# Mixing layer: mask adds and sums of squares moved from GpSimd to VectorE, rotated keys copied by ScalarE

## The chip, the cores and the metric

The kernel runs on one core of a Trainium2 chip. The metric is the device time of one execution in microseconds (us); the median of several runs counts. A core has five engines that each work through a queue of their own in order: TensorE (PE in the profile, its weight loads PEld), VectorE (DVE), ScalarE (ACT), GpSimd (POOL) and SyncE (SP). Transfers between the chip's main memory and the on-chip buffers run on 16 DMA engines; here SyncE issues nearly all of them (the weights, queue q1), ScalarE a few small tables (q10), and GpSimd the rest (q0).

## The reference, cut to what matters

The program is two transformer blocks in float32 over 256 tokens of width 1024. The first block, with its experts, is not touched. The second is a feed-forward layer, a mixing layer and a second feed-forward layer. The mixing layer, where the change lies, computes

```python
z = rms_norm_2(h, mix_pre_g[l]) @ w_in[l]
q_na, k_na, v_na, c_q, c_kv, k_rope = jnp.split(z, split_at, axis=-1)
o_na = neighbourhood_attention(q_na, k_na, v_na, na_rpb[l])      # 8 heads of 64
o_mla = latent_attention(c_q, c_kv, k_rope, ...)                 # 8 heads of 64 + 32 rotated
mixed = concat([rms_norm_2(o_na, g1), rms_norm_2(o_mla, g2)]) @ w_out[l]
h = h + rms_norm_2(mixed, mix_post_g[l])
...
bias = rpb[:, row_off, col_off]                    # in neighbourhood_attention
bias = jnp.where(col_mask, bias, NEG_INF)          # the mask
s = einsum(q, k) * D ** -0.5 + bias
...
k_rot = apply_rope(k_rope, cos, sin)               # in latent_attention: one key for all heads
s = (einsum(qn, k_nope) + einsum(qr, k_rot)) * scale
```

## The kernel before, in words

Every matrix product is made of three matmuls: both operands are split into a rounded high part and a low part (H and L in the names), and HH, LH and HL are summed (lines 116 to 118). ScalarE makes the high parts of weights (wH) and VectorE the low parts (wL), just ahead of TensorE, from three buffers each. Tokens come in two halves, tt = 0 and 1, of 128.

The mixing layer is the function mix. In the order of the code: small tables are loaded (gains, rope tables, the window table win of 128x64 that holds 0 or -1e30); then for each of four pairs of heads, hp, a bias table G of 128 x (2 heads x 6 x 64) is gathered from rpb in four loads of GpSimd's queue and the window is added to it in place on GpSimd (line 1758). The first three G have buffers of their own, the fourth lies in the buffer of a row that the feed-forward layer before it uses last. Then z for its last 416 columns (pslin from za and zb, the preloaded weights, into zr); late, the factor of the row norm of each half, which reaches TensorE through diag and psrr; the values vn from w_in columns (L1559 for their low parts); the norms of the two latent parts (rstd chains of small VectorE steps, then xh); the products with mla_w_uq (wuq) and mla_w_ukv (wukv); the rotation (rope, on VectorE), whose shared key kr GpSimd copies to 8 heads in mqk (line 1828). Then three streams are woven: the projections of q_na and k_na (pslt), the latent attention pairs, and the neighbourhood pairs (near), in which TensorE adds G to the scores by a matmul with ident (line 1876). The function attend does softmax and output of a pair; its last steps square the output on ScalarE into sqt (line 2029) and, from the second pair on, add it to the running sum sq on GpSimd (line 2031). After the last pair four small matmuls (pssq) reduce sq to the norm factors of the output.

What sets the order: a scheduler walks the instructions by priority, mostly the order of the code, with a model of its own of when each is ready, and writes down a fixed queue for every engine except SyncE, whose loads stay in the order of the code. So an instruction that is written late in the code can be placed early where the model sees its engine free. At run time each engine takes its queue strictly in order and waits at each instruction for semaphores. A DMA signals its end on one of eight counters for loads of SyncE and ScalarE (DMAHW0 to 7) or one of eight for loads of GpSimd (DMASW0 to 7), taken in turn; a load can't be issued before the earlier load on the same counter has landed. The window table, on ScalarE's queue, has the counter of wukv, on SyncE's.

Of the kernel before, what the change touches and what calls it, by code (L numbers as in the profile page):

```python
# [15 lines left out]
ALU = mybir.AluOpType  # L16
# [4 lines left out]
P = 128  # L21
# [83 lines left out]
class Net:  # L105
# [1621 lines left out]
    def mix(self):  # L1727
        nc, tc, a = self.nc, self.tc, self.a
        H, L = self.H, self.L
        with ExitStack() as es:  # L1730
# [11 lines left out]
            win = pool.tile([P, 64], F32, name="win")  # L1742
# [3 lines left out]
            biases = []  # L1746
            for hp in range(4):
                if hp < 3:
                    G = pool.tile([P, 2, 6, 64], F32, tag="G", name="G", bufs=3)
                else:  # L1750

                    G = self.pc.tile([P, D], F32, tag="row", name="G")[:, 0:768].rearrange("p (a r c) -> p a r c", a=2, r=6)
                for j, half in itertools.product(range(2), range(2)):
                    src = bass.AP(tensor=rpb.tensor, offset=rpb.offset + (2 * hp + j) * 465 + (5 - half) * 31 - 48,
                                  ap=[[1, 64], [31, 6], [1, 64]])
                    nc.gpsimd.dma_start(G[half * 64:half * 64 + 64, j], src)
                G = G.rearrange("p a r c -> p (a r) c")
                nc.gpsimd.tensor_tensor(G, G, win[:, None, :].to_broadcast([P, 12, 64]), op=ALU.add)
                biases.append(G)
            W = a["w_in_2"]  # L1760

            def into(t, n, late=False):
# [25 lines left out]
            for tt in range(2):  # L1788
                t = pool.tile([P, P], F32, tag="diag", name="diag", bufs=2)
# [15 lines left out]
            q, kk = qk[:, 0], qk[:, 1]  # L1805
# [17 lines left out]
            for tt in range(2):  # L1823
                c, s = rope[:, tt, 0], rope[:, tt, 1]
                self.rope(q[:, tt, :, 64:96], q[:, tt, :, 64:96], c, s, 8)
                kr = pool.tile([P, 1, 32], F32, tag="kr", name="kr", bufs=2)
                self.rope(kr, zr[:, tt, None, 384:416], c, s, 1)
                nc.gpsimd.tensor_copy(kk[:, tt, :, 64:96], kr.to_broadcast([P, 8, 32]))

            def projections():  # L1830
                for t, c0, scale, rev in ((qn, 0, 0.125, 64), (kn, 512, 1.0, 0)):
# [6 lines left out]
            sq = [pool.tile([P, S], F32, tag=f"sq{i}", name=f"sq{i}") for i in range(2)]  # L1838
# [25 lines left out]

            def near(hp):
                G = biases[hp]
                yield
                ss = [self.ps.tile([P, 2, S], F32, tag="wk", name="psna") for _ in range(2)]
                for tt in range(2):
                    for j in range(2):  # L1870
                        hs = slice(j * 64, j * 64 + 64)
                        nc.tensor.matmul(ss[j][:, tt], qn[hs, hp, tt * P:(tt + 1) * P], kn[hs, hp, :],
                                         start=tt == 0, stop=False, skip_group_check=True)
                for j in range(2):
                    for tt in range(2):
                        nc.tensor.matmul(ss[j][:, tt], self.ident, G[:, 6 * j + 2 - 2 * tt:6 * j + 6 - 2 * tt, :],
                                         start=False, stop=tt == 1, skip_group_check=True)
                yield
                yield from self.attend(ss, [self.att_p() for _ in range(2)], 1.0, lambda kb, j: vn[:, kb, (2 * hp + j) * 64:(2 * hp + j) * 64 + 64],
                                       hp, *outs[0], gout[0], sq[0], 64)  # L1880
# [6 lines left out]
            def latent_out():  # L1887
                for j in range(2):
                    yield from self.linear_steps(*outs[1], 4, ws[0][j], 512,
                                                 lambda tt, ps: nc.scalar.copy(z1[tt][j], ps), "ln", 2)  # L1890

            weave([projections(), wait(5), latent_out()], [latent(0), latent(2), near(0), near(2)],
                  [wait(2), latent(1), latent(3), near(1), near(3)])

            parts = []
# [11 lines left out]
            r = None  # L1907
            for tt in range(2):
                z0 = {}
                for j in ((0, 1), (1, 0))[tt]:  # L1910
# [6 lines left out]
                    if r is None:  # L1917
# [8 lines left out]
                        with tc.high_priority():  # L1926
                            nc.vector.tensor_scalar(v, ps, 4.0 / 512, 4 * EPS, op0=ALU.mult, op1=ALU.add)
                            r = self.rstd_wide(pool, v)
# [57 lines left out]
    def attend(self, s, p, scale, v, hp, oH, oL, g, sq, rev):  # L1986

        nc, pool = self.nc, self.pa  # L1990
        m = pool.tile([P, 2, 4], F32, tag="attm", name="attm", bufs=2)
        for j in range(2):
            nc.vector.tensor_reduce(m[:, j, 0:2], s[j], axis=AX.X, op=ALU.max, negate=True)
        if scale != 1.0:
            nc.vector.tensor_scalar(m[:, :, 0:2], m[:, :, 0:2], scale, None, op0=ALU.mult)
        yield
        for j in range(2):
            for tt in range(2):
                nc.scalar.activation(p[j][:, tt], s[j][:, tt], AF.Exp, bias=m[:, j, tt:tt + 1], scale=scale,
                                     accum_out=m[:, j, 2 + tt:3 + tt])  # L2000
        nc.vector.reciprocal(m[:, :, 2:4], m[:, :, 2:4])
        for j in range(2):
            for tt in range(2):
                nc.vector.tensor_scalar(p[j][:, tt], p[j][:, tt], m[:, j, 2 + tt:3 + tt], None, op0=ALU.mult)
        yield
        pT = []
        for j in range(2):
            pt = self.ps.tile([P, 2, S], F32, tag="wk", name="pspt")
            for kb in range(2):
                for tt in range(2):  # L2010
                    nc.tensor.transpose(pt[:, kb, tt * P:(tt + 1) * P], p[j][:, tt, kb * P:(kb + 1) * P], self.ident)
            t = pool.tile([P, 2, S], F32, tag="attT", name="attT", bufs=4)
            nc.scalar.copy(t, pt)
            pT.append(t)
        yield
        po = self.ps.tile([P, S], F32, tag="wk", name="pspo")
        for kb in range(2):
            for j in range(2):
                nc.tensor.matmul(po[j * 64:j * 64 + 64], v(kb, j), pT[j][:, kb], start=kb == 0, stop=kb == 1,  # L2019
                                 skip_group_check=True)  # L2020
        t = sq if hp == 0 else pool.tile([P, S], F32, tag="attT", name="sqt", bufs=4)
        h, lo, o, o2 = oH[:, hp], oL[:, hp], po, t
        if rev:
            o, h, lo, o2 = (u.rearrange("p (g r) -> p g r", r=rev) for u in (o, h, lo, o2))
            o = o[:, :, ::-1]
        gk = g[:, hp:hp + 1]
        nc.scalar.activation(h, o, AF.Copy, scale=gk)
        nc.vector.scalar_tensor_tensor(lo, o, gk, h.bitcast(F32), op0=ALU.mult, op1=ALU.subtract)
        nc.scalar.activation(o2, o, AF.Square)
        if hp:  # L2030
            nc.gpsimd.tensor_tensor(sq, sq, t, op=ALU.add)
        yield


# [47 lines left out]
```

## Time and profile before

| what | value |
|---|---|
| median of 3 runs | 1282.73 us (1282.36 to 1283.06) |
| profiled execution, own time | 1284.1 us |
| its span, first to last instruction | 1282.3 us |
| TensorE busy | 1199.6 us, 94% |
| VectorE busy | 704.2 us, 55% |
| ScalarE busy | 550.6 us, 43% |
| GpSimd busy | 36.2 us, 3%, 43 instructions |
| granted clock of TensorE | 0.990 of full speed |
| main memory read | 349.46 MB, 273 GB/s over the span |

The mixing layer takes the stretch from about 950 to 1085 us of the span, after the experts (to about 720 us) and the first feed-forward layer of the second block. Times in the rows below count from the span's start. A TensorE row that reads "[1.30 <-DVE diag L1790]" says that TensorE stood idle for 1.30 us before this instruction and that VectorE's instruction of line 1790, which writes diag, ended the wait.

### The profile page before, as it was taken

The page shows a single profiled execution, that of the slowest core. Times are in us where ns is not written, and L with a number is a line of the kernel's source. Part 1 is how long each engine was busy: PE and PEld are TensorE (multiplying, and loading weights), DVE is VectorE, ACT ScalarE, POOL GpSimd, SP SyncE. Part 2 cuts the span into 40 slices and gives each one's busy share as a digit, 9 for nine tenths or more (in the row PEclk, how much of TensorE's full clock was granted, in tenths as well). Part 3 has the DMA queues.
Part 4 walks back from the last instruction along what each step waited for, and adds up shares of the span by engine and source line. Part 5 has one row for each costly group of instructions (what it writes and reads, how often), then busy time and mean ns, then how long its engine had stood idle before and what let it go on. Part 6 is the DMA issues. An engine that isn't in the chain of part 4 may idle for free. (4 is left out here: it accounts for less than half of the span.)

```text
span 1282.3 us, 19860 instructions
## 1 busy us (share of the span) xinstructions
PE 1199.6 (94%) x7213; PEld 817.4 (64%) x7213; DVE 704.2 (55%) x1570; ACT 550.6 (43%) x1056; POOL 36.2 (3%) x43
## 2 busy tenths in 40 slices
PE   5999999999899899899879989999998998999997
PEld 3885788775354344335335447888876976788885
DVE  3565888774343233133323257667769767666664
ACT  3466765642121111011112146556635675555652
POOL 0000000000000000000000000000024000000000
PEclk9999999999999899899999999999999999999999
DMA  9886767789999999999999994953397114195510
GB/s 332 273 289 209 286 209 269 259 318 406 402 409 408 407 408 409 409 408 409 408 407 409 403 330 154 322 197 133 136 267 155 34 64 134 66 367 186 187 66 33
DMA packets 155140, 351.85 MB, mean 274 GB/s; under 512 B 14688, under 2 KB 69920, under 8 KB 155040
## 3 DMA queue, kind: packets, MB, share of 16 engines
q1 hardware_dynamic: 152816, 347.25, 73.1%
q0 software_dynamic: 1328, 3.16, 1.9%
q8 instruction: 58, 0.95, 0.3%
q14 instruction: 42, 0.34, 0.1%
q10 hardware_dynamic: 896, 0.15, 0.1%
HBM read 349.46 MB, written 1.06 MB: 273 GB/s over the span
## 5 line engine op out<-in xcount | busy, mean ns | idle before, releaser
L1337 PE MATMUL psgu<-wgu,xg 128*32 128x512 f32 x1600 | 215.1, 610 | 32.8 <-DMA wgu<-in_w_up_e_dram 32.0
L1337 PEld LDWEIGHTS psgu<-wgu,xg 128*32 128x32 f32 x1600 | 64.4, 112 | 175.5 <-issue 147.9
L1559 DVE SCALAR_TENSOR_TENSOR wL<-wgu,ffn_pre_g,wH 128x512 fp32r<-128x512 f32 x160 | 119.0, 751 | 72.5 <-ACT wH L1558 68.5
L1558 ACT ACTIVATE wH<-wgu,ffn_pre_g 128x512 fp32r<-128x512 f32 x160 | 114.2, 724 | 78.2 <-PE psgu L117 71.9
L116 PE MATMUL psgu<-wH,Hc 128*128 128x512 f32 x320 | 126.2, 394 | 0.0
L118 PE MATMUL psgu<-wL,Hc 128*128 128x512 f32 x320 | 124.9, 390 | 0.0
L117 PE MATMUL psgu<-wH,Lc 128*128 128x512 f32 x320 | 124.7, 390 | 0.0
L1344 DVE SCALAR_TENSOR_TENSOR act<-act,ws,psgu 128x256 f32<-128x256 f32 x25 | 12.0, 481 | 188.4 <-ACT act L1343 188.4
L1361 PE MATMUL psdn<-wdn,aT 128*32 128x512 f32 x800 | 93.4, 595 | 3.5 <-DVEq L1096 2.0
L1343 ACT ACTIVATE act<-psgu 128x256 f32<-128x256 f32 x25 | 9.6, 384 | 200.7 <-PE psgu L1337 200.7
L125 ACT CAST wH<-gt 128x512 fp32r<-128x512 f32 x61 | 37.7, 618 | 117.3 <-DVE gt L1197 106.0
L126 DVE TENSOR_TENSOR wL<-win,wH 128x512 fp32r<-128x512 f32 x80 | 54.0, 688 | 32.2 <-ACT wH L125 30.4
L118 PEld LDWEIGHTS psgu<-wL,Hc 128*128 128x128 f32 x320 | 60.1, 188 | 12.7
L117 PEld LDWEIGHTS psgu<-wH,Lc 128*128 128x128 f32 x320 | 60.1, 188 | 12.2
L116 PEld LDWEIGHTS psgu<-wH,Hc 128*128 128x128 f32 x320 | 60.1, 188 | 12.0
L126 DVE TENSOR_TENSOR wL<-gt,wH 128x512 fp32r<-128x512 f32 x61 | 42.2, 692 | 41.6 <-ACT wH L125 41.5
L125 ACT CAST wH<-win 128x512 fp32r<-128x512 f32 x80 | 48.2, 617 | 32.5 <-PE pslt L118 17.1
L1361 PEld LDWEIGHTS psdn<-wdn,aT 128*32 128x32 f32 x800 | 24.7, 109 | 53.6 <-issue 44.3
L1311 ACT ACTIVATE xg<-psga,sh,gs 128x256 f32<-128x256 f32 (+1 forms) x52 | 28.8, 556 | 66.1 <-PE psga L1310 66.1
L126 DVE TENSOR_TENSOR wL<-wdn,wH 128x512 fp32r<-128x512 f32 x64 | 44.1, 693 | 22.2 <-ACT wH L125 11.7
L125 ACT CAST wH<-wdn 128x512 fp32r<-128x512 f32 x64 | 39.5, 620 | 27.3 <-PE fy L117 18.8
L1309 PE MATMUL psga<-Pt,xH 128*128 128x256 f32 (+1 forms) x208 | 51.1, 288 | 0.0
(548 smaller groups left out, 2525.2 us busy)
## 6 DMA issues: line engine op xcount, KB each, us to landing
wgu<-in_w_gate_e_dram SPq DMA_DIRECT2D x128, 512.0 KB, 12.0
wgu<-in_w_up_e_dram SPq DMA_DIRECT2D x128, 512.0 KB, 12.0
wdn<-in_w_down_e_dram SPq DMA_DIRECT2D x62, 1024.0 KB, 12.1
wgu<-in_ffn_w_gu_dram SPq DMA_DIRECT2D x88, 512.0 KB, 6.7
win<-in_w_in_dram SPq DMA_DIRECT2D x26, 1024.0 KB, 12.2
wada<-in_w_ada_dram SPq DMA_DIRECT2D x24, 1024.0 KB, 7.7
wdn<-in_ffn_w_down_dram SPq DMA_DIRECT2D x22, 1024.0 KB, 9.2
wout<-in_w_out_dram SPq DMA_DIRECT2D x8, 1024.0 KB, 14.3
```

What stands on the lines that cost most here:

```text
L116: mm(ps, lH, rH, start=start, stop=False, skip_group_check=True)
L117: mm(ps, lL, rH, start=False, stop=False, skip_group_check=True)
L118: mm(ps, lH, rL, start=False, stop=stop, skip_group_check=True)
L125: self.nc.scalar.copy(H, raw)
L126: self.nc.vector.tensor_sub(L, raw, H.bitcast(F32))
L1309: mm(o, xH[:, tt, k + kk], pt, start=kk == 0 and tt == 0, stop=False, skip_group_check=True)
L1311: nc.scalar.activation(B.xg[:, k, :w], ps[:, 0, :w], AF.Identity, scale=self.gs2[:, k:k + 1], bias=self.sh2[:, k:k + 1])
L1337: mm(ps[q:q + 32], xg[:, k, i * P + q:i * P + q + 32], W[e][:, :, k % 4, :], start=k == 0, stop=k == 7)
L1344: nc.vector.scalar_tensor_tensor(act, act, ws[:, i:i + 1], ps[:, 1], op0=ALU.mult, op1=ALU.mult)
L1361: mm(ps[q:q + 32], aT[:, f, q:q + 32], wd[e][:, f, sl], start=f == 0, stop=f == 1)
L1558: self.nc.scalar.activation(H, raw, AF.Copy, scale=g)
L1559: self.nc.vector.scalar_tensor_tensor(L, raw, g, H.bitcast(F32), op0=ALU.mult, op1=ALU.subtract)
```

## The change

Three kinds of instruction leave GpSimd. The window is added to G on VectorE, at the head of near, the function that uses G, instead of where G is loaded. The rotated key is copied to the eight heads by ScalarE. The squares are summed on VectorE. GpSimd keeps its loads.

```diff
                     nc.gpsimd.dma_start(G[half * 64:half * 64 + 64, j], src)
-                G = G.rearrange("p a r c -> p (a r) c")
-                nc.gpsimd.tensor_tensor(G, G, win[:, None, :].to_broadcast([P, 12, 64]), op=ALU.add)
-                biases.append(G)
+                biases.append(G.rearrange("p a r c -> p (a r) c"))
...
                 self.rope(kr, zr[:, tt, None, 384:416], c, s, 1)
-                nc.gpsimd.tensor_copy(kk[:, tt, :, 64:96], kr.to_broadcast([P, 8, 32]))
+                nc.scalar.copy(kk[:, tt, :, 64:96], kr.to_broadcast([P, 8, 32]))
...
             def near(hp):
                 G = biases[hp]
+                nc.vector.tensor_tensor(G, G, win[:, None, :].to_broadcast([P, 12, 64]), op=ALU.add)
                 yield
...
         if hp:
-            nc.gpsimd.tensor_tensor(sq, sq, t, op=ALU.add)
+            nc.vector.tensor_tensor(sq, sq, t, op=ALU.add)
```

The fixed queues move with it. Line numbers of the changed kernel are one or two lower. On GpSimd, at the head of the mixing layer, the loads of G stand between the four adds before:

```order
L1756 DMA G<-in_na_rpb_dram 64x6x64 [waits DMASW5_49]
L1756 DMA G<-in_na_rpb_dram 64x6x64 [waits DMASW6_49]
L1758 TENSOR_TENSOR G<-G,win 128x768 [waits DMASW4_49,DMASW3_49,DMAHW1_49,DMASW2_49,DMASW1_49]
L1756 DMA G<-in_na_rpb_dram 64x6x64 [waits DMASW7_49]
L1756 DMA G<-in_na_rpb_dram 64x6x64 [waits DMASW0_49]
L1756 DMA G<-in_na_rpb_dram 64x6x64 x2
L1758 TENSOR_TENSOR G<-G,win 128x768 [waits DMASW6_49,DMASW7_49,DMASW5_49,DMASW0_49]
```

and of the changed kernel, from the same load on:

```order
L1756 DMA G<-in_na_rpb_dram 64x6x64 [waits DMASW5_49]
L1756 DMA G<-in_na_rpb_dram 64x6x64 [waits DMASW6_49]
L1756 DMA G<-in_na_rpb_dram 64x6x64 [waits DMASW7_49]
L1756 DMA G<-in_na_rpb_dram 64x6x64 [waits DMASW0_49]
L1756 DMA G<-in_na_rpb_dram 64x6x64 [waits DMASW1_49]
L1756 DMA G<-in_na_rpb_dram 64x6x64 [waits DMASW2_49]
L1756 DMA G<-in_na_rpb_dram 64x6x64 [waits DMASW3_49]
L1756 DMA G<-in_na_rpb_dram 64x6x64 [waits DMASW4_49]
L1756 DMA G<-in_na_rpb_dram 64x6x64 [waits DMASW5_49,DVE_49,Pool_49]
```

Each load now waits for the load eight places earlier, and the thirteenth for the row's buffer too, where an add and its wait for the window table (DMAHW1) stood. On VectorE, at the step that follows the features of the second half (Lc), the first add comes ahead of the two rstd chains, of which one (nss_9040) gives late and the other xh:

```order
 L1553 TENSOR_TENSOR Lc<-pspn,Hc 128x4x128 x2
+L1865 TENSOR_TENSOR G<-G,win 128x768
+L140 TENSOR_SCALAR rstd<-nss_9040 128x1
 L142 TENSOR_SCALAR rstd<-nss 128x1
 L155 TENSOR_SCALAR rstd<-rstd 128x1
 L144 TENSOR_SCALAR rstd<-rstd 128x1
```

The second add stands after zr of the second half, the third and fourth among the weight splits and latent norms that follow; none is left to the attention. On ScalarE, where the projections begin, the two copies of the key come in:

```order
+L1901 CAST wHL<-wout_9368 128x512 x3
+L1826 COPY mqk<-kr 128x8x32
+L1558 ACTIVATE wH<-win_9388,mix_pre_g_695 128x512
+L1826 COPY mqk<-kr 128x8x32
+L1558 ACTIVATE wH<-win_9390,mix_pre_g_695 128x512
+L1850 COPY qkT<-psqk 96x512
```

Each copy stands ahead of a weight cast wH of the projections.

## Rows read from the trace of the kernel before

**Rows 1.** The page: busy time, share of the span, instructions of each engine.

```profile
PE 1199.6 (94%) x7213; PEld 817.4 (64%) x7213; DVE 704.2 (55%) x1570; ACT 550.6 (43%) x1056; POOL 36.2 (3%) x43
```

**Rows 2.** By stage: length, busy PE, PEld, DVE, ACT, POOL, PEclk, DMA share, GB/s.

```profile
950.00:1000.00 50.00, 41.31 (x233) 36.20 (x232) 44.81 (x130) 26.29 (x56) 15.80 (x16) 1.00 0.76 192
1000.00:1050.00 50.00, 49.89 (x324) 41.48 (x324) 36.42 (x79) 36.53 (x95) 2.21 (x3) 1.00 0.04 13
```

**Rows 3.** Waits of TensorE, 950 to 1000 us: us in total, times, longest.

```profile
PE pslt L117 <- DVE wL L1559: 3.0, 2, 1.5
PE pslin L116 <- ACT Hc L1551: 2.0, 1, 2.0
...
PE pslin L118 <- DVE wL L126: 1.1, 1, 1.1
PE pslin L118 <- DVE rstd L156: 0.8, 1, 0.8
PE psqk L1848 <- POOL mqk L1828: 0.4, 1, 0.4
```

**Rows 4.** Timeline of TensorE: start, length, what, [idle before <-releaser].

```profile
964.11 0.49 PE L1791 MATMUL psrr<-diag,ones 128*128 128x128 f32 x2 [1.30 <-DVE diag L1790]
```

**Rows 5.** The chain that ended last, in order of time: start, length.

```profile
932.00 21.95 DMA wukv<-in_mla_w_ukv_dram
953.97 5.45 DMA win<-in_window_dram
```

**Rows 6.** Timeline of ScalarE, two places.

```profile
954.36 1.95 ACT L1558 ACTIVATE wH<-win,mix_pre_g 128x512 fp32r<-128x512 f32 x3 [3.70 <-DMA wukv<-in_mla_w_ukv_dram]
...
983.39 0.37 ACT L1820 COPY mqk<-pslin 128x256 f32<-128x256 f32 x1
```

**Rows 7.** Timeline of GpSimd: loads of G and the first mask add.

```profile
934.25 3.94 POOL L1756 DMA_DIRECT2D G<-in_na_rpb_dram  x6 [2.51 <-PE psgu L118]
959.59 1.84 POOL L1758 TENSOR_TENSOR G<-G,win 128x768 f32<-128x768 f32 x1 [21.39 <-DMA win<-in_window_dram]
961.37 2.62 POOL L1756 DMA_DIRECT2D G<-in_na_rpb_dram  x4
```

**Rows 8.** Timeline of VectorE: four long rows, three plain ones, an rstd pair.

```profile
959.69 1.76 DVE L146 SCALAR_TENSOR_TENSOR rstd<-rstd 128x1 f32<-128x1 f32 x1
...
962.24 0.57 DVE L241 TENSOR_SCALAR xh<-zr,rstd 128x256 f32<-128x256 f32 x1
...
965.56 0.75 DVE L1559 SCALAR_TENSOR_TENSOR wL<-win,mix_pre_g,wH 128x512 fp32r<-128x512 f32 x1 [1.11 <-PE pslin L118]
...
969.34 1.81 DVE L241 TENSOR_SCALAR xh<-zr,rstd 128x256 f32<-128x256 f32 x1
...
978.38 0.55 DVE L126 TENSOR_TENSOR wL<-wuq,wH 128x384 fp32r<-128x384 f32 x1
...
979.67 1.97 DVE L126 TENSOR_TENSOR wL<-wuq,wH 128x384 fp32r<-128x384 f32 x1
...
989.45 2.31 DVE L1559 SCALAR_TENSOR_TENSOR wL<-win,mix_pre_g,wH 128x512 fp32r<-128x512 f32 x1
...
1086.17 0.21 DVE L140 TENSOR_SCALAR rstd<-nss 128x1 f32<-128x1 f32 x1
...
1088.29 0.15 DVE L1575 COPY late<-rstd 128x1 f32<-128x1 f32 x1
```

**Rows 9.** DMA queues, 954 to 962, then 966 to 986: packets, MB, share.

```profile
q1 hardware_dynamic: 1424, 2.82, 99.1%
...
q0 software_dynamic: 420, 0.86, 56.3%
q1 hardware_dynamic: 1281, 2.53, 38.3%
```

**Rows 10.** Issue to landing: the sixth load of G with its neighbour; the rope table.

```profile
DMA to landing us min/median/max: 13.5/14.4/15.3
...
rope<-in_rope_dram ACTq DMA_DIRECT2D x1, 32.0 KB, 7.4
```

## The prediction

> **What bounds the kernel now.** I read four views in this order. The page's busy line [rows 1] says TensorE is busy 94% of the span, so the question is where its other 6% lies near the edit. The table by stage [rows 2] answers: from 950 to 1000 us, the head of the mixing layer, TensorE has 41.31 of 50 us, and from 1000 to 1050, where its attention runs, 49.89 of 50. So an edit counts between 950 and 1000, and additions to VectorE or ScalarE in the next 50 us are free as long as TensorE stays full. The waits of TensorE [rows 3, 4] give the 8.7 us of idle time piece by piece: 2.0 for Hc from ScalarE, 1.3 for diag from VectorE at 964.11, then 0.8, 1.1 and twice 1.5 for VectorE, 0.4 for the rotated key that GpSimd copies. VectorE is busy 44.81 of these 50 us: it is the second bound. The chain [rows 5] shows where the 2.0 comes from: the window table's load, on ScalarE's queue, can't be issued before wukv, a load of SyncE, has landed at 953.95 (their completions share a counter), and everything behind it on ScalarE stands still, 3.70 us of it in front of wH [rows 6], then Hc.
>
> VectorE's own rows [rows 8] hold a second finding. Four of its instructions take far longer than the same form elsewhere: 1.76 us for a 128x1 step whose like takes 0.2, 1.81 against 0.57, 1.97 against 0.55, 2.31 against 0.75. They start at 959.69, 969.34, 979.67 and 989.45, within 0.6 us of the four mask adds of GpSimd (the first at 959.59, 1.84 us [rows 7]; the others go in the same 10 us steps). So each mask add already blocks VectorE for about 1.6, 1.2, 1.4 and 1.6 us. The second, third and fourth sum to 4.2.
>
> **The change part by part, after the order of the changed kernel.**
>
> *1. Four mask adds on VectorE.* The trace has no such row. 128x384 with two SBUF inputs takes 0.55 [rows 8]; twice the columns cost between 0.55 and 1.1, I take 0.95, pitch 0.9. They don't wait for their pair's turn: the order puts all four into the head, ahead of the work that TensorE waits for there. Call T the time at which TensorE gets diag (964.11 before [rows 4]). The first add stands ahead of both rstd chains. It can start when the window table has landed, S (before 953.97 + 5.45 = 959.4, 959.6 on GpSimd). Behind it two chains woven together take 2.1 us up to late (1086.17 to 1088.29 [rows 8]), then xh, 0.5 of its 0.57, and diag, by the same rows some 0.4 with the handing over: T = S + 0.9 + 2.1 + 0.1 + 0.5 + 0.4 = S + 4.0 or 4.1. Before, T was S + 4.5, because the block sat inside the chains. So with S unmoved T comes 0.4 earlier.
>
> *2. After T.* The second add falls into 1.11 us in which VectorE idles at 965.56, the third and fourth cost 0.9 each in a busy stretch, and the blocks of 4.2 are gone: VectorE gains 4.2 - 1.8 = 2.4 by 991 us. TensorE's waits after T are 5.3 us. Of these 0.8, 1.1 and the second 1.5 stand right behind a block; the 0.4 goes with GpSimd's copy. I take 2.4 + 0.4, and 0.2 since the chain through all four adds to the copied key is cut: -3.0 in all. Bounds: -1.8 if the order's new places for weight splits cost a us, -3.8 if all four waits vanish.
>
> *3. The mask loads.* This is the term against the change. GpSimd issues in order. Before, six of the 16 loads of G go out from 934.25 and the other ten wait behind mask adds, from 961.37 on [rows 7]. Now nothing stands between them but the rotating counters: two more go out at about 938, the third pair's four as the first four land, the last four from the landing of the fifth on, 936.9 + 13.5 = 950.4. The six of before had all landed at 937.5 + 15.3 = 952.8 [rows 10], just ahead of wukv; now the queue stays full into the 970s. What a full G queue does to weight loads the trace shows: from 954 to 962 without G the weight queue moved 2.82 MB in 8 us, 353 GB/s; from 966 to 986 beside G it moved 2.53 MB in 20 us, 127 GB/s [rows 9], with loads outstanding throughout. Until 952.8 the engines that finish last were serving G in both versions. wukv's 0.52 MB takes 1.5 us at the one rate, 4.1 at the other: +2.6. The upper bound is one packet of each queue in turn: a G packet took 56.3% x 16 x 20 us / 420 = 0.43 us, a weight packet 99.1% x 16 x 8 / 1424 = 0.089, so weights would keep 17% and wukv land 1.5 / 0.17 - 1.5 = 7.3 later. The lower bound is 0: wukv could be ahead of the new loads in all engines. I take 3.3, near the measured rate. The window table then travels beside G: 5.45 before, 7.4 for the rope table issued while G was still running [rows 10]; I take 6.2, +0.7. So S moves by 4.0, and T by 4.0 - 0.4 = +3.6. The wait for Hc grows by the same 3.3, but lies ahead of T and is not counted twice. The later masks' loads: G moved 0.86 MB in the 20 us of [rows 9], 8.7 loads, 2.3 us each, so the ten land by 952.8 + 23 = 976; VectorE reaches the fourth add about 10 us after T, near 978. That is close, but no term.
>
> The Trainium skill ("DMA: Bandwidth & Descriptors", section on queues, rings and completion order) says each DMA engine takes the queues with work in turn, a whole packet at a time. By that alone the upper bound would hold; the 127 GB/s of the trace speak for a milder share, and the sum goes by the trace.
>
> *4. Keys copied by ScalarE.* Two copies at about 0.4 each (0.37 for 128x256 [rows 6]). Each waits for kr from VectorE, and behind them stand the weight casts wH of the projections and then the qkT copy. VectorE finishes both kr over 2 us earlier once the blocks are gone, ScalarE is busy 26.29 of 50 us there [rows 2]: 0, at most +0.7.
>
> *5. Six sums of squares on VectorE.* At about 0.4 (below the 0.55 of 128x384), 2.5 us. Five lie where TensorE is full or VectorE waits for ScalarE; VectorE has 36.42 of 50 us [rows 2]. The last stands ahead of the final scale, which waits for TensorE anyway: 0, at most +0.5; not below -0.4, since nobody waits for the GpSimd version in the trace.
>
> **Sum.** +3.6 - 3.0 + 0 + 0 = +0.6 us against the profiled span of 1282.3. The execution took 1284.1, 1.8 outside the span, and is 1.4 above the median of the runs, 1282.73; the outside doesn't change, so the forecast is 1282.7 + 0.6 = 1283.3. A measurement of this kernel can tell about 0.2%, 2.6 us, from no change.
>
> **The rivals.**
>
> *A, forecast: the freed VectorE pays for the crowded DMA queues.* 1283.3; with 2.6 to 4.2 us on wukv and the bounds of step 2 it runs from 1281 to 1285. For it: both sizes are measured in this trace. Chance 0.45.
>
> *B, faster: wukv isn't held up.* If the new loads stay behind wukv in the engines that finish last (they are issued 6 us and more after it), S stays, T gains 0.4 and the rest 3.0 to 3.8: 1279.3 to 1278.5. Against it: the last G load of before, issued 5.5 us after wukv, landed ahead of it [rows 5, 10]. It decides when the delay of S stays below about 0.8 us. Chance 0.28.
>
> *C, slower: the window table is held up in full.* At the place of step 3, by the price of the upper bound: wukv +7.3, less what loads finish meanwhile, say +5.5 to 7.3, and the table +0.7. T moves by 5.8 to 7.6, the sum is +2.8 to +4.6: 1285.5 to 1287.3. It decides from an S later by about 6 us. For it: beside G the weights had 38.3% of the engines' time and G 56.3% [rows 9]. Against it: that is twice the 17% of strict turns. Chance 0.22.
>
> *D: the change frees nothing.* Were the long rows of VectorE not GpSimd's doing, four adds would be pure addition, 3.6 us, on top of step 3: +7, 1290. Four coincidences of four speak against it. Chance 0.05.
>
> **Numbers.** Faster by over 0.2% (under 1280.2): B, 0.28. Within: A, 0.45. Slower (over 1285.3): C and D, 0.27. The range reaches from inside B to inside C, 1278.8 to 1286.8, and leaves out some 0.1 on either side.
>
> **What the new profile would show.** VectorE's four long rows gone and four adds at 0.95 us: step 2 right. wukv landing near 957 instead of 953.95, the window table near 963.5, the first add right behind it, diag near 967.7, and G landing without a gap up to 975: step 3 right. TensorE's waits: Hc 5 us, diag 1 to 2, those of VectorE after it 2 to 3 us together instead of 5. Wrong would be: a wait for G itself in front of an add, a wait of ScalarE for the projections' weights (their loads queue behind wout's, now slower), or new waits after 1000 us.

## The result, and the profile after

The changed kernel is slower: 1291.51 us median of 8 runs (1287.04 to 1295.86) against 1282.55 us of the kernel before beside it. The medians lie 9.0 us apart; the ratio over all runs is 1.0056, 95% interval 1.0039 to 1.0072, some 7 us (5 to 9). A second set of runs, shown below, gave 1.0039 (1.0024 to 1.0054). The forecast was 1283.3, the upper end of the range 1286.8.

The page's busy line and the table by stage of the changed kernel (columns as in [rows 1, 2]):

```profile
PE 1202.8 (93%) x7213; PEld 822.1 (64%) x7213; DVE 702.5 (54%) x1580; ACT 551.5 (43%) x1058; POOL 22.6 (2%) x31
```

```profile
950.00:1000.00 50.00, 38.27 (x186) 33.02 (x184) 36.63 (x131) 23.42 (x54) 3.29 (x5) 0.88 0.67 197
1000.00:1050.00 50.00, 49.95 (x342) 42.85 (x342) 38.03 (x79) 34.50 (x86) 0.00 (x0) 0.99 0.07 22
```

GpSimd has 13.6 us less to do than in [rows 1], VectorE is no busier. The loss lies in the head: TensorE has 38.27 of 50 us (41.31 in [rows 2]), and its clock is no longer full, 0.88 against 1.00. The attention behind it is as full as before. TensorE's waits from 950 to 1000 (total, times, longest) answer to [rows 3, 4]:

```profile
PE psrr L1789 <- DVE diag L1788: 8.2, 1, 8.2
PE pslin L116 <- ACT Hc L1551: 1.6, 1, 1.6
PE pslt L117 <- DVE wL L1559: 1.0, 1, 1.0
PE psqk L1846 <- DVE mqk L1977: 0.8, 1, 0.8
```

The waits behind diag have shrunk from 5.3 to 1.8 us, as forecast; the one for diag has grown from 1.3 to 8.2. The chain (start, length), which answers to [rows 5], tells why:

```profile
954.93 14.47 DMA win<-in_window_dram
969.53 0.96 DVE G L1865
...
972.73 0.29 DVE diag L1788
973.06 0.79 PE psrr L1789 x2
```

VectorE's row of that add says the same:

```profile
969.53 0.96 DVE L1865 TENSOR_TENSOR G<-G,win 128x768 f32<-128x768 f32 x1 [8.91 <-DMA win<-in_window_dram]
```

The window table travels for 14.47 us instead of 5.45. The first mask add waits for it on VectorE, the rstd chains stand behind the add, diag behind the chains. The DMA issues from 930 to 960 (KB each, median us to landing) show that the weights were not the ones held up: wukv lands in 19.2 us, before in 21.95.

```profile
wukv<-in_mla_w_ukv_dram SPq DMA_DIRECT2D x1, 512.0 KB, 19.2
rope<-in_rope_dram ACTq DMA_DIRECT2D x1, 32.0 KB, 14.5
win<-in_window_dram ACTq DMA_DIRECT2D x1, 32.0 KB, 14.5
```

GpSimd's loads of G go out as the order said: eight at once, four one by one, the last four when the row's buffer is free (compare [rows 7]).

```profile
936.68 5.27 POOL L1756 DMA_DIRECT2D G<-in_na_rpb_dram  x8 [2.51 <-PE psgu L118]
943.48 0.66 POOL L1756 DMA_DIRECT2D G<-in_na_rpb_dram  x1 [1.53 <-DMA G<-in_na_rpb_dram]
...
954.36 2.63 POOL L1756 DMA_DIRECT2D G<-in_na_rpb_dram  x4 [3.59 <-DVE rstd L156]
```

A second cost appears on TensorE's own timeline. Same shape, same operands, but right behind the wait the matmuls start every 0.43 us (their pitch), and from 977.5 on every 0.23:

```profile
973.06 0.79 PE L1789 MATMUL psrr<-diag,ones 128*128 128x128 f32 x2 [8.23 <-DVE diag L1788]
...
974.08 0.63 PE L116 MATMUL pslin<-wH,Hc 128*128 128x512 f32 x1
974.51 0.63 PE L117 MATMUL pslin<-wH,Lc 128*128 128x512 f32 x1
...
977.70 0.39 PE L116 MATMUL pslin<-wH,Hc 128*128 128x512 f32 x1
977.93 0.39 PE L117 MATMUL pslin<-wH,Lc 128*128 128x512 f32 x1
```

The granted clock of the same stretch (third column from the right) has gone to its lower level, 1.2 GHz, and comes back:

```profile
960.00:965.00 5.00, 4.83 (x26) 4.37 (x24) 0.62 (x2) 1.42 (x6) 0.00 (x0) 1.00 1.07 219
965.00:970.00 5.00, 0.00 (x0) 0.00 (x0) 0.47 (x1) 0.00 (x0) 0.00 (x0) 0.72 1.03 360
970.00:975.00 5.00, 1.94 (x6) 1.65 (x7) 4.59 (x26) 1.07 (x5) 0.00 (x0) 0.50 0.94 347
975.00:980.00 5.00, 5.00 (x18) 3.99 (x17) 3.23 (x15) 2.47 (x5) 0.00 (x0) 0.76 0.29 88
```

**Where the 9.5 us between the two profiled spans (1282.3 and 1291.8) lie.** The first load of G, which stands ahead of everything the change touches, starts 2.4 us later (936.68 against 934.25); that is scatter of the first 930 us (in the runs below it starts anywhere from 934.38 to 938.16). From there to the matmul on diag the changed kernel takes 36.4 us, before 29.9: +6.5. From that matmul to the end it takes 318.7, before 318.2: +0.5. The split compares like with like: TensorE has 132 or 133 instructions between the two points in both kernels.

### The profile page after: what moved, and what is told of

It is laid out like the page before. It is cut to its first block, busy times and chain, and to the rows that moved or that the text cites. A ratio compares the mean times of both kernels' runs of the same rounds, so it can differ in the third digit from the quotient of the medians.

```text
span 1291.8 us, 19839 instructions
## 1 busy us (share of the span) xinstructions
PE 1202.8 (93%) x7213; PEld 822.1 (64%) x7213; DVE 702.5 (54%) x1580; ACT 551.5 (43%) x1058; POOL 22.6 (2%) x31
```

## Experiments

Each set of runs has its own runs of the kernel before beside it; the ratios compare. "To diag" is the time from the first load of G to the matmul on the second diag, "rest" from there to the end of the span, both in us of one profiled execution, which took 1.1 to 2.6 us more than the median of its runs, in e7 4.8. "Table" is the window table's time from issue to landing.

| kernel | table | mask adds | to diag | rest | ratio, 95% interval |
|---|---|---|---|---|---|
| before | 5.5 | GpSimd, between the loads | 29.9 | 318.2 | 1 |
| changed | 14.5 | VectorE, in the head | 36.4 | 318.7 | 1.0056 (1.0039 to 1.0072) |
| e5 changed, again | 14.6 | same | 37.3 | 318.6 | 1.0039 (1.0024 to 1.0054) |
| e1 table early | early | same | 27.1 | 316.4 | 0.9939 (0.9921 to 0.9957) |
| e2 adds at their turn | 12.3 | VectorE, in the attention | 30.3 | 314.5 | 0.9957 (0.9939 to 0.9975) |
| e8 both | early | VectorE, in the attention | 27.4 | 314.8 | 0.9949 (0.9934 to 0.9964) |
| e12 table first in its queue | 7.2 | VectorE, in the head | 27.8 | 317.9 | 0.9972 (0.9959 to 0.9986) |
| e3 loads held back | 7.3 | VectorE, in the head | 28.3 | 325.2 | 1.0028 (1.0016 to 1.0040) |
| e4 before, loads first | 13.8 | GpSimd, behind the loads | 27.0 | 322.1 | 1.0015 (1.0002 to 1.0028) |
| e7 before, table early | early | GpSimd, between the loads | 28.9 | 325.8 | 1.0001 (0.9989 to 1.0012) |
| e11 e4 and e7 | early | GpSimd, behind the loads | 35.6 | 314.2 | 1.0008 (0.9995 to 1.0022) |
| e10 only copies and sums moved | 5.4 | GpSimd, between the loads | 30.6 | 318.9 | 0.9994 (0.9979 to 1.0009) |

### e5: the changed kernel again

> The changed kernel once more, unaltered, as the yardstick for the three runs beside it and for a second profile. Theory (the wait for the window table, 14.5 us in the first profile, is the cost, and the clock falls in the stretch behind it): the table lands over 10 us after its issue again, TensorE's wait for diag is 4 to 9 us, the granted clock is below 0.9 in the 10 us after that wait, time 0.4 to 0.7% above the kernel before. Rival (the first profile was a bad one): wait below 3 us, clock at its upper level, under 0.3%.

1290.72 us, 1.0039. The table took 14.6 us, diag was waited for 6.9 us, and behind it the clock was low again (stage table, 970 to 980):

```profile
970.00:980.00 10.00, 7.09 (x23) 5.77 (x24) 7.91 (x42) 3.55 (x10) 0.00 (x0) 0.66 0.50 163
```

So the first profile was no accident, though the ratio came out at the lower end of what was expected.

### e1: the table loaded early

```diff
@@ where the pools of the feed-forward layers are set up
+            self.win = pc.tile([P, 64], F32, name="win")
+            self.nc.scalar.dma_start(self.win, self.a["window"])
@@ mix
-            win = pool.tile([P, 64], F32, name="win")
-            nc.scalar.dma_start(win, a["window"])
+            win = self.win
```

> The changed kernel with one edit: the window table is loaded at the start of the first feed-forward layer instead of at the head of the mixing layer. Theory (the first mask add, placed ahead of the rstd chains on VectorE, waited for a window table that took 14.5 us beside the loads of G): the add starts right behind Lc, TensorE's wait for diag falls from 8.2 to under 1.5 us, the clock stays at its upper level from 960 to 990, and the time is 1278.5 to 1281. Rival 1 (the crowded queues hold up other loads too, weights above all): 1284 to 1288 with new waits of ScalarE for weights. Rival 2 (the adds as work of VectorE are the cost): no gain over the changed kernel, 1289 to 1292.

1277.54 us, 0.9939: the wait was the whole loss, and more. All waits of TensorE from 925 to 1050:

```profile
PE pslt L117 <- DVE wL L1561: 1.0, 1, 1.0
PE psqk L1847 <- DVE mqk L1978: 0.8, 1, 0.8
PE pspn L1550 <- DVE x L1599: 0.4, 2, 0.3
PE pspo L2019 <- ACT attT L2013: 0.2, 1, 0.2
```

None for Hc, none for diag. VectorE's first add starts 1.3 us after Lc began and holds up nobody, and the clock from 970 to 980 is full with TensorE busy throughout:

```profile
956.40 1.35 DVE L1555 TENSOR_TENSOR Lc<-pspn,Hc 128x512 fp32r<-128x512 f32 x2
957.67 0.95 DVE L1866 TENSOR_TENSOR G<-G,win 128x768 f32<-128x768 f32 x1
```

```profile
970.00:980.00 10.00, 10.00 (x53) 8.54 (x52) 9.51 (x25) 7.57 (x17) 0.00 (x0) 1.00 0.76 281
```

Rival 1 (crowded queues hold up other loads as such) and rival 2 (the adds as work of VectorE) fall: loads and adds are those of the changed kernel. The gain was more than the theory had; TensorE no longer waits for Hc either (1.6 us in the changed kernel).

### e2 and e8: the adds at their pair's turn

```diff
-                nc.vector.tensor_tensor(G, G, win..., op=ALU.add)
+                tc.keep_in_program_order(
+                    nc.vector.tensor_tensor(G, G, win..., op=ALU.add))
```

> The changed kernel with one edit: each mask add is pinned behind the VectorE work emitted before it, so that the four adds run at their pair's turn in the attention (near 1010 to 1040 us) and not in the head. The loads are as in the changed kernel. Theory (it was the place of the first add): the window table still takes about 14 us, but nobody in the head waits for it; diag goes to TensorE some 3 us earlier than in the kernel before, clock at its upper level, 1278 to 1280.5. Rival 1 (crowded queues as such): 1284 to 1288. Rival 2 (adds as work of VectorE, now in a stage with VectorE at 36 of 50 us): TensorE waits up to 4 us in the attention, 1282 to 1284.

> The changed kernel with both edits: the window table early, and each mask add pinned to its pair's turn. Theory: with the table early the place of the adds matters little, VectorE is busy 34 to 39 of 50 us in the attention and the adds are covered there; in the head VectorE has 3.6 us less: 0.55 to 0.8% faster than the kernel before, the best of the versions. Rival (in the attention an add holds back the maxima and the scaling of the probabilities, and so TensorE): 0.3 to 0.5%, slower than with the early table alone.

e2 gave 0.9957, e8 0.9949. In e2 the table is still late (12.3 us), but the first add stands here now:

```profile
1026.20 0.94 DVE L1866 TENSOR_TENSOR G<-G,win 128x768 f32<-128x768 f32 x1
```

and TensorE waits neither for diag nor for anything in the attention. That settles that it was the adds' place in the head, the first ahead of the rstd chains, and not the table's lateness by itself. Diag didn't come 3 us earlier, as the theory had it: 30.3 us against 29.9, with 2.4 us for Hc ahead of it and a clock of 0.88 from 960 to 970. The gain lies behind diag, 314.5 against 318.2. With the table early, e8 is no better than e1 (the intervals overlap): four adds of 0.95 us cost nothing measurable in either place. Rival 2 of e2 and the rival of e8 fall.

### e12: the table first in its own queue

```diff
+            win = pool.tile([P, 64], F32, name="win")
+            nc.scalar.dma_start(win, a["window"])
             gq = self.gain(pool, a["mla_q_norm_g_2"], 2, "gq")
...
             nc.scalar.dma_start(rope, a["rope"].rearrange(...))
-            win = pool.tile([P, 64], F32, name="win")
-            nc.scalar.dma_start(win, a["window"])
```

> The changed kernel with the four small loads of ScalarE's queue in another order: the window table first, then the two latent gains and the rope table; in the changed kernel it was the last of the four. Loads of G, adds and the order of every other engine are the same. It goes out about 2 us earlier and asks why it took 14.5 us. Theory 1 (each small piece waits its turn behind pieces of G and of the weights, and the table stood behind the pieces of three other small loads in its own queue): with nothing ahead of it the table lands 4 to 8 us after its issue, near 960; TensorE's wait for diag is under 2 us, 0.3 to 0.6% faster than the kernel before. Theory 2 (any small load takes long beside G, whatever stands ahead of it in its queue): 11 to 15 us again, landing near 966, wait for diag 4 to 6 us, within 0.3% of the kernel before or up to 0.4% slower.

0.9972. The loads of G and the order on TensorE and VectorE are those of the changed kernel. The same four small loads, from 930 to 990:

```profile
win<-in_window_dram ACTq DMA_DIRECT2D x1, 32.0 KB, 7.2
rope<-in_rope_dram ACTq DMA_DIRECT2D x1, 32.0 KB, 13.6
...
gq<-in_mla_q_norm_g_dram ACTq DMA_DIRECT2D x1, 1.0 KB, 9.9
gkv<-in_mla_kv_norm_g_dram ACTq DMA_DIRECT2D x1, 0.5 KB, 12.6
```

The table now lands in 7.2 us beside the same crowd, and the gain of 0.5 KB behind it needs 12.6. So what theory 2 forecast didn't come: going out last of four small loads in one queue, while the G queue was full, is what made 14.5 us of it. Whether the pieces ahead of it did that (theory 1) or its later start, e12 doesn't part, since the table also went out 2.5 us earlier, counted from the first load of G, and so 1.9 us ahead of the last four loads of G (953.75) instead of just behind their start. For the place speaks that the queue as a whole was done no sooner: its last load lands 32.2 us after that first load of G (rope, 968.3), in the changed kernel 32.7 (the table). In the other runs with eight loads of G at once, too, the first of the small loads, the norm gain gq of 1 KB, took 6.8 to 11.3 us and the last 12.3 to 15.1. For the start speaks e7: there gq, with nothing ahead of it in its queue, goes out just behind four loads of G (950.33 and 949.88) and takes 12.9.

The wait for diag is gone, and two lines in another order turn a loss of 0.4 to 0.6% into a gain of 0.3% (0.1 to 0.4%).

What one small piece pays beside G was not measured by itself. The Trainium skill ("DMA: Bandwidth & Descriptors", section on queues, rings and completion order) says that each DMA engine goes round the queues that have work, a packet at a time. This case doesn't decide how far that carries: from 954 to 970 of the changed kernel the trace counts 1948 packets of the weight queue, 704 of the small loads and 297 of G, but it doesn't show that every queue had work on every engine throughout, nor that its packets are those of the page.

### e3: the later loads of G held back

```diff
                 biases.append(G.rearrange("p a r c -> p (a r) c"))
+                if hp == 0:
+                    gate = pool.tile([P, 1], F32, name="gate")
+                    nc.gpsimd.tensor_copy(gate, win[:, 0:1])
```

(with the order of GpSimd pinned).

> The changed kernel with one edit: after the first four loads of G, GpSimd copies one column of the window table, so that the other twelve loads go out only when the table has landed, somewhat as in the kernel before. The adds stay on VectorE, ahead of the rstd chains. Theory (the loads of G made the table late): the table lands 5 to 7 us after its issue, T is within 1 us of the kernel before, and what the adds on VectorE freed remains: 1279.5 to 1282.5. If the table is late for another reason: 14 us again and 1289 to 1292. If the later masks now come too late for the second to fourth add: waits of VectorE for G, 1284 to 1290.

1.0028. The first half of the theory holds: with only four loads of G ahead of it, the table took 7.3 us (last of the four again), and the matmul on diag came 1.5 us earlier than in the kernel before. The time went the third way, masks that come too late for VectorE. First and second add:

```profile
959.96 0.96 DVE L1870 TENSOR_TENSOR G<-G,win 128x768 f32<-128x768 f32 x1 [1.82 <-DMA win<-in_window_dram]
969.77 0.96 DVE L1870 TENSOR_TENSOR G<-G,win 128x768 f32<-128x768 f32 x1 [5.76 <-DMA G<-in_na_rpb_dram]
```

VectorE stands 5.76 us before the second add; TensorE waits 4.6 us for the weight split behind it. An add that the order puts into the head makes every load that it needs critical, G as well as the table.

### e4, e7, e11: loads and table moved, adds left on GpSimd

```diff
-                G = G.rearrange("p a r c -> p (a r) c")
-                nc.gpsimd.tensor_tensor(G, G, win..., op=ALU.add)
-                biases.append(G)
+                biases.append(G.rearrange("p a r c -> p (a r) c"))
+            for G in biases:
+                tc.keep_in_program_order(nc.gpsimd.tensor_tensor(G, G, win..., op=ALU.add))
```

That is e4; e7 is the kernel before with the diff of e1; e11 has both.

> The kernel before with one edit: GpSimd issues all 16 loads of G ahead of its four mask adds; the adds, the key copies and the sums stay on GpSimd. So the queues are as crowded as in the changed kernel, but no VectorE instruction waits for the window table. Theory (the crowding costs only by way of the add ahead of the rstd chains): the window table takes 10 to 15 us, TensorE's wait for diag stays under 1.5 us, the time is within 0.2% of the kernel before, 1281 to 1284. Rival (crowding as such, by weights that come later): 1285 to 1290.

> The kernel before with one edit: the window table loaded at the start of the first feed-forward layer; mask adds, key copies and sums stay on GpSimd. It tells how much of the gain of the early table belongs to the table and how much to the work taken off GpSimd. Theory (GpSimd's adds block VectorE for over a us each wherever they run): the adds go out as the loads of G land, from about 950, and block VectorE there; gain 1 to 3 us against the kernel before (the wait of ScalarE ahead of the first weight cast goes, T comes earlier by up to 2), 0.1 to 0.25%, clearly less than the 0.6% of the changed kernel with the same edit. Rival (the table is all that matters): 0.5 to 0.7%.

> The kernel before with the window table early and all 16 loads of G ahead of the mask adds; adds, key copies and sums stay on GpSimd. Against the changed kernel with the early table (0.6% faster than before) it differs only in who does the elementwise work. Theory (each add on GpSimd holds up VectorE by over a us): four long rows of VectorE right behind one another, begun as soon as the last but two loads allow, 957 to 970, which puts up to 5 us into the rstd chains and the weight splits; 0.0 to 0.3% faster than the kernel before. Rival (the early loads and the early table are the whole gain): 0.5 to 0.7% faster.

1.0015, 1.0001, 1.0008: none of them gains anything. e4 stayed within the expected bound, but for another reason than the theory's: diag came early, and the loss lay behind it. Its four adds on GpSimd, and VectorE's timeline beside them:

```profile
970.24 7.18 POOL L1760 TENSOR_TENSOR G<-G,win 128x768 f32<-128x768 f32 x4 [11.79 <-DMA win<-in_window_dram]
```

```profile
970.29 1.95 DVE L241 TENSOR_SCALAR xh<-zr,rstd 128x256 f32<-128x256 f32 x1
972.15 1.77 DVE L149 SCALAR_TENSOR_TENSOR rstd<-rstd 128x1 f32<-128x1 f32 x1
...
973.96 1.79 DVE L241 TENSOR_SCALAR xh<-zr,rstd 128x128 f32<-128x128 f32 x1
...
975.79 2.17 DVE L1559 SCALAR_TENSOR_TENSOR wL<-win,mix_pre_g,wH 128x512 fp32r<-128x512 f32 x1
```

Four adds in a row, four long rows in a row: VectorE gets these four and three short ones done in 7.6 us (970.29 to 977.9), and TensorE waits 5.5. In e11 three adds in a row catch one single instruction, a weight split that elsewhere takes 0.75:

```profile
957.30 5.32 POOL L1761 TENSOR_TENSOR G<-G,win 128x768 f32<-128x768 f32 x3
```

```profile
957.25 5.93 DVE L1561 SCALAR_TENSOR_TENSOR wL<-win,mix_pre_g,wH 128x512 fp32r<-128x512 f32 x1 [1.45 <-ACT wH L1560]
```

TensorE waits 6.8 us right behind it. In e7, where the adds stand between the loads of G again, the last loads go out at 970 and what is late are weights of the projections: ScalarE waits 4.29 us for them ahead of 986.09, TensorE 1.8 and 2.8. (This profile is of the slowest of e7's twelve runs; its rest of 325.8 is too high to set beside the ratio.)

```profile
986.09 0.72 ACT L1560 ACTIVATE wH<-win,mix_pre_g 128x512 fp32r<-128x512 f32 x1 [4.29 <-DMA win<-in_w_in_dram]
```

e7's theory had wanted 0.1 to 0.25% and got nothing. Against e1, e11's code differs only in who does the elementwise work, and e1 is 0.7% faster. So the gain needs both: the adds off GpSimd, and nobody ahead of diag who waits for the table.

### e10: only copies and sums moved

The changed kernel with the mask adds back on GpSimd as before.

> The changed kernel with one part undone: the mask adds go back to GpSimd, between the loads of G as in the kernel before; what stays of the change is the two key copies on ScalarE and the six sums on VectorE. Theory (these two parts cost and bring next to nothing): within 0.1% of the kernel before, TensorE's wait for the key copied by GpSimd (0.4 us) gone, no new wait over 0.5 us in the attention. Rival (the sums hold VectorE up where the probabilities are scaled): 0.1 to 0.3% slower with new waits of TensorE between 1020 and 1060.

0.9994, no difference beyond the interval (0.9979 to 1.0009). The attention shows no new wait of TensorE, the one for the key copied by GpSimd is gone.

### e6 and e9: TensorE kept busy through the wait

```diff
-            rps = self.ps.tile([P, S], F32, tag="wk", name="psrr")
+            rps = self.ps.tile([P, 2, S], F32, tag="wk", name="psrr")
+            idle, rps = rps[:, 1], rps[:, 0]
             for tt in range(2):
                 ...
+                for i in range(28 * tt):
+                    tc.keep_in_program_order(nc.tensor.matmul(idle[:, 0:P], self.ones, self.ident, ...))
```

e9 has 40 instead of 28. The trace counts each of them twice.

> The changed kernel with 28 extra matmuls of TensorE (ones by identity, into a part of the PSUM tile that nobody reads), which stand between the projections of the second half and the one that waits for diag, so that TensorE works through most of that wait. The extra work moves some later instructions on VectorE and ScalarE too. Theory (the clock falls because TensorE stood idle): diag comes as late as before the edit, but the granted clock in the 20 us behind it stays at 1.00 and the work there takes its usual time; that is worth 2 to 3 us against the changed kernel. Rival (the clock falls for another reason, in power or in the DMA load): the clock falls as in the changed kernel, and the time is the same or longer by what the extra matmuls outlast the wait, up to 2 us.

> As the run with 28 extra matmuls, with 40: at 0.23 us each, as those 28 took, they last about 9.2 us, and the wait they stand in was 5.97 + 3.63 = 9.6 us there. With 28, TensorE still idled 3.6 us and the clock fell to 0.66 in the next 10 us all the same. Theory (idle time of TensorE brings the clock down): no idle time is left, the clock stays at 1.00 from 960 to 1000, and the work behind T takes 2 to 3 us less than with 28: 0.2 to 0.4% above the kernel before. Rival (something else brings it down): the clock falls below 0.9 in 970 to 980 again, 0.4 to 0.7% above the kernel before.

The times say little (1.0051 with an interval of 1.0037 to 1.0065, and 1.0064 with 1.0040 to 1.0088): the extra work moved VectorE's order, and in e9 a new wait of 4.1 us for a weight split came up. By the numbers the rival fits both: no time gained, and a clock of 0.66 (e6) and 0.89 (e9) from 970 to 980. The theory's times failed. But the rows inside that stretch of e9 hold both cases side by side:

```profile
961.74 8.65 PE L1792 MATMUL psrr<-ident,ones 128*128 128x128 f32 x76
970.23 0.39 PE L1794 MATMUL psrr<-diag,ones 128*128 128x128 f32 x2
...
970.92 0.39 PE L118 MATMUL pslin<-wL,Hc 128*128 128x512 f32 x1
971.14 0.39 PE L116 MATMUL pslin<-wH,Hc 128*128 128x512 f32 x1
...
977.99 0.80 PE L118 MATMUL pslin<-wL,Hc 128*128 128x512 f32 x1 [4.12 <-DVE wL L1559]
978.58 0.63 PE L116 MATMUL pslin<-wH,Hc 128*128 128x512 f32 x1
979.01 0.63 PE L117 MATMUL pslin<-wH,Lc 128*128 128x512 f32 x1
```

Where the extra matmuls fill the wait for diag, the work behind it goes on at a pitch of 0.23 us. Where TensorE stands idle for 4.1 us, some 4 us later in the same run, the pitch behind it is 0.43. In e6 the extra matmuls ended early, 3.6 us of idle time were left, and the clock from 970 to 980 was 0.66 as in e5. So behind the long waits of these traces the low clock follows TensorE's idle time. Behind shorter ones it is not uniform: 1.00 from 955 to 965 behind the 2.0 us for Hc in the kernel before, 0.66 from 960 to 965 behind 2.4 us for Hc in e5. What it costs by itself no run measured, since neither kept the rest in place.

## Why the prediction was wrong, step by step

**1. The adds on VectorE** were right. They take 0.95 to 0.96 us, all four stand in the head, and the matmul on diag comes 3.7 us after the table has landed (973.06 - 969.40), where 4.0 or 4.1 were forecast.

**2. What VectorE gains** was right in size. The long rows of [rows 8] are gone, and TensorE's waits after diag fell by 3.5 us (5.3 to 1.8; forecast -3.0). That GpSimd's adds block VectorE was an inference from four coincidences; e4 and e11 show it with adds in a row, up to 5.93 us for one instruction. Rival D falls with it.

**But the gain didn't arrive**, and that is the second thing that failed: a term that the prediction put at nothing. From diag to the end the profile shows +0.5 instead of -3.0, since TensorE's clock was low for part of it. The share of the clock missing in each stretch, times TensorE's busy time there, is an estimate of the cost: 1.0 (970 to 975) and 1.2 us (975 to 980) right behind the wait for diag, and 0.8 in a dip from 990 to 1000 that e5 has too. The pitch alone gives 1.6 for the eight matmuls at 0.43 instead of 0.23. Counted in stretches of 2.5 us from diag to the end, the estimate is 5.3 us (e5: 5.1; the kernel before: 0.0). Without it the rest would be 313.4 (e5: 313.5) against 318.2: VectorE's gain is there, and the clock took it. Only a part of that belongs to the wait for diag. By the same count e12, whose TensorE doesn't wait for diag, loses 4.8 us and e1 3.3, all of e1's and 3.1 of e12's between 1050 and 1100; e2 and e8 lose nothing, and their rest is 314.5 and 314.8. What brings the later dips, and why only in some profiles, no run shows. The prediction had no term for the clock: it read 1.00 in [rows 2] and took it as given.

**3. The mask loads** is the step that failed, in its last link. The sum had +3.3 for wukv and +0.7 for the table's own transit. Measured between the profiles: the table is issued 1.5 us earlier (954.93 - 953.97, less the 2.4 of scatter), so wukv cost nothing (the wait for Hc, forecast at 5 us, was 1.6), and the transit is +9.0. With the 1.0 us that diag comes sooner behind the table, that makes the +6.5, where +3.6 was forecast. It is as near as that only by luck: wukv was put 4.8 us too high and the transit 8.3 too low. The sentence that failed is "I take 6.2, +0.7". It was bounded by the rope table's 7.4 us [rows 10], which flew when the six loads of G had all but landed (952.8); the nearest row of a load beside a full G queue stood in the same group, G's own 13.5 to 15.3. And the table's place was not asked for: it is the fourth of four small loads in ScalarE's queue, and with the table first e12 has 7.2 us in place of 14.5. Of the 8.9 us between the forecast's +0.6 and the 9.5 of the two profiled spans, 2.4 are scatter ahead of the change, 2.9 are this step, and 3.5 are the gain of step 2 that didn't arrive.

**4 and 5. Copies and sums**: no effect that e10 can tell from nothing, 0.9994 (0.9979 to 1.0009).

**The rivals.** C had the right outcome (slower, by a table that is held up) and the wrong link (wukv). The +6.5 up to diag lies inside its 5.8 to 7.6; its 1285.5 to 1287.3 was still below what came, since it too counted on the 3.0 us of step 2. B's premise, wukv not held up, was met, but not its condition, an S delayed by less than 0.8 us, since B let the table go with wukv. D's 1290 came nearest to the measured time, by luck: VectorE was freed, against its premise. The forecast's sign that would refute it, a wait in front of an add, was named for G and came for the table.

**What stays open.** Why e1 is ahead of e12 by 0.3%: its table saves 0.7 us up to diag and the 1.4 us for Hc that lie in it, and e12 had a clock of 0.83 from 980 to 990 in its profile (8.13 us busy, 1.4 us); the rest isn't accounted for. Open, too, is whether the table's place or its earlier start made e12's 7.2 us, and what lowers the clock between 1050 and 1100 in some profiles.

## What to carry to other kernels

When work moves to a busier engine, look at what it will stand in front of there, and at every load that it waits for: on GpSimd a late table held up only masks that nobody needed yet, on VectorE it held up the chain to TensorE. A small load's time depends on which queues are full beside it and on when its turn comes in its own, so a bound for it should come from a row with the same neighbours; put the load that a chain waits for first. And ask what TensorE's clock does behind a wait that grows: the row that read 1.00 was taken without that wait. Elementwise work on GpSimd was paid by VectorE, and taking it away was worth 0.3 to 0.6% here, but only once the chain to TensorE no longer waited for the table.

## What was not expected of the hardware

- TensorE's granted clock fell to its lower level behind waits of TensorE: pitch 0.43 us instead of 0.23 behind 8.2 us (changed kernel) and behind 4.1 us (e9), while the same stretch ran at 0.23 where other matmuls had filled the wait (e9). Such a wait thus cost more than its own length, 1.6 us by the pitch in the changed kernel.
- A load of 32 KB took 5.4 (e10) to 15.1 us (e6) depending on what else was queued, and one of 0.5 KB took 12.6 us as third in its queue (e12).
- One VectorE instruction that usually takes 0.75 us lasted 5.93 us beside three adds of GpSimd (e11).
